# Delta-rule operands on VectorE, bonus products a step later, merged gram masks, and 62 instead of 82 products ahead of the block inverses

## Chip, cores and metric

One Trainium2 chip, one core. The metric is the device time of one execution in microseconds (us). The time before is 968.35 us, the median of 3 runs (964.66 to 969.06).

## What is computed

One layer of a hybrid encoder on 1024 tokens of width 1024, in float32. A normalised input goes through one combined projection (3724 columns), whose pieces feed four branches: A, an mLSTM matrix memory (4 heads of 64); B, causal pooling over trailing windows; C, RWKV-7 time mixing, a delta rule with data-dependent decay; D, forgetting attention. The gated branches are joined by an output projection, and a cross-attention into 256 memory tokens follows. The change touches branch C and, in two small places, branch A:

```python
def step(state, xs):                      # branch C, for every token
    r_t, k_t, v_t, w_t, kk_t, a_t = xs
    sa = jnp.einsum("bhvk,bhk->bhv", state, -kk_t)
    state = state * w_t[:, :, None, :] + sa[..., None] * (kk_t * a_t)[:, :, None, :] \
            + v_t[..., None] * k_t[:, :, None, :]
    return state, jnp.einsum("bhvk,bhk->bhv", state, r_t)
...
bonus = jnp.sum(rh * kh * bonus_u, axis=-1, keepdims=True) * vh
```

## The kernel before

Float32 accuracy comes from three passes: both factors of a product are split into a high and a low part, and a **product** is three matmuls (L137 to L139, hi*hi, lo*hi, hi*lo). A product of the projections has 512 moving columns, or 260 to 264 for the two value projections (`vgemm`).

TensorE's order is the order in which the program is written (`manual_schedule`). The large projections are generators in a list of fillers; `fill(n)` takes n units from the list and puts them at that place in TensorE's stream. A 512-column product counts one unit, a `vgemm` product half a unit. So the small dependent steps of branch C stand in TensorE's queue with fixed numbers of products between them. The other engines' order is set by a scheduler with priorities.

Branch C has these stages, in this order:

- **Preparation** (`cprep`, L512 to L555), one step for each of two halves of the sequence (`hf`) and two pairs of heads (`j`), four steps in all. A step begins on TensorE with the two gate products (tiles `sm`, written by L137 to L139 from `lora` and `sp`); ScalarE takes two tanh (L525, L529); VectorE makes a running sum (L533); ScalarE two exponentials (L535, L537); then the operands are written: `EE` (tiles `t`, `ee`) and `BK` (tile `bk`) by L546 to L549, each on 64 partitions x 512 elements. L546 and L548 run on VectorE, L547 and L549 on GpSimd. L550 makes the input of the bonus on VectorE. After a `yield`, TensorE sums it over channels (L554, the **bonus product**) and VectorE copies the result (L555). The buffers `gc`, `ep`, `ta` and `km` exist once, so a step's first ScalarE operation waits until the step before has read them. The PSUM tiles `sm` have two buffers, used in turn.
- **Gram blocks** (`cgram`, L562): 128 small matmuls (L570) in eight groups; VectorE multiplies each result by a mask (L577, L579) on its way out of PSUM.
- **Inverses** (`cinv`, L588): the masked blocks go to DRAM (`dN`, L585) and come back in another layout (L590); VectorE runs 31 dependent steps (L597, L599) that invert 128 blocks of 32 x 32; the result goes to DRAM (`dTn`, `dTt`, L601, L602) and is read back (L611 to L613) by `tinv`, whose first matmul is L621. Meanwhile TensorE takes `fill(NI)`, `NI = 82`: the projections DQ and DK with the norms of their heads (`rgemm`, L805, L806), and most of the value projection AV.
- **Chain** (`cchain`, L663): 16 dependent steps with up to six units between their parts; what is left of the fillers comes after.

Then the mLSTM: `mpre(i)` (L1024) makes the weights of a block from `e`, loaded from `cd` (L1030), and products L1037; `mlstm(i)` (L1041) has the products L1052 with the state. Both have 64 rows of contraction: the halves of the partitions (`PH[x]`) are two heads.

The transfers in question all stand in SyncE's one queue, in order.

Of the kernel before, what the change touches and what calls it, by code (L numbers as in the profile page):

```python
# [36 lines left out]
def tile_trunk(ctx: ExitStack, tc: tile.TileContext, a, out, dbg=None):  # L37
# [317 lines left out]
    masks = []  # L355
# [157 lines left out]
    def cprep(hf, j):  # L513
        hs, js = slice(hf * 512, (hf + 1) * 512), slice(j * 128, (j + 1) * 128)
        cr, ck = shifted[j], shifted[2 + j]
        if j == 0:
            BON[hf] = cm("bon", [128, 4, 4])
            EG[hf] = cm("eg", [128, 2, 8])
        bk = cm("bk", [128, 8, 2, 64])
        BK[j][hf] = bk  # L520
        ep = c1("ep", [128, 8, 65])
        p = ps("sm", [128, 512])
        mm3(p, lora[0][0:64, js], lora[1][0:64, js], cwa[0][0:64], cwa[1][0:64], True, True)
        gc = c1("gc", [128, 512])
        SC.activation(gc, p, AF.Tanh, bias=col(36 + j), scale=0.5)  # L525
        p = ps("sm", [128, 512])
        mm3(p, lora[0][64:128, js], lora[1][64:128, js], cwa[0][64:128], cwa[1][64:128], True, True)
        ta = c1("ta", [128, 512])
        SC.activation(ta, p, AF.Tanh, bias=col(38 + j), scale=0.5)  # L529
        if hf == 0 and j == 1:  # L530
            csplit(1)
        V.tensor_scalar(gc, gc, 1.0, None, op0=ALU.add)
        V.tensor_tensor_scan(gc, smask.rearrange("p a b -> p (a b)"), gc, 0.0, op0=ALU.mult, op1=ALU.add)  # L533
        G.memset(ep[:, :, 0:1], 1.0)
        SC.activation(ep[:, :, 1:65], v3(gc), AF.Exp, scale=-CDEC)  # L535
        V.tensor_copy(EG[hf][:, j, :], ep[:, :, 64])
        act["cprep"] = SC.activation(gc, gc, AF.Exp, scale=CDEC)  # L537
        kk = KN.pop((hf, j))
        km = c1("km", [128, 512])
        V.tensor_scalar(km, ta, pd[:, 7 + j:8 + j], pd[:, 9 + j:10 + j], op0=ALU.mult, op1=ALU.add)  # L540
        V.tensor_tensor(km, ck[:, hs], km, op=ALU.mult)
        V.scalar_tensor_tensor(ta, ta, 1.0, gc, op0=ALU.add, op1=ALU.mult)
        for x in range(2):
            r = PH[x]
            e = EE[x][hf][r, j]
            V.scalar_tensor_tensor(e[:, :, x, :], v3(kk[r]), -1.0, ep[r, :, 0:64], op0=ALU.mult, op1=ALU.mult)  # L546
            G.tensor_tensor(e[:, :, 1 - x, :], v3(cr[r, hs]), ep[r, :, 1:65], op=ALU.mult)  # L547
            V.scalar_tensor_tensor(bk[r, :, x, :], v3(kk[r]), 0.5, v3(ta[r]), op0=ALU.mult, op1=ALU.mult)  # L548
            G.tensor_tensor(bk[r, :, 1 - x, :], v3(km[r]), v3(gc[r]), op=ALU.mult)  # L549
        V.scalar_tensor_tensor(kk, cr[:, hs], col(44 + j), km, op0=ALU.mult, op1=ALU.mult)  # L550
        yield
        bps = ps("sm", [128, 4, 2])
        for i in range(4):
            T.matmul(bps[:, i, :], kk[:, i * 128:(i + 1) * 128], ones2, start=True, stop=True)  # L554
        V.tensor_copy(BON[hf][:, :, 2 * j:2 * j + 2], bps)  # L555
# [4 lines left out]
    def cgram(hf, n):  # L560
        bq = cc("bq", [128, 8, 2, 128])
        BQ[hf] = bq  # L562
        for cp in range(4):
            pp = [ps(t_, [128, 2, 2, 128]) for t_ in (("cw", "cs") if cp % 2 else ("sm", "sm"))]
            for j in range(2):
                for c2 in range(2):
                    c = cp * 2 + c2
                    for x in range(2):
                        r = PH[x]
                        T.matmul(pp[x][:, j, c2, :], BK[j][hf][r, c].rearrange("p a b -> p (a b)"),  # L570
                                 EE[x][hf][r, j, c].rearrange("p a b -> p (a b)"), start=True, stop=True)
            fill(n)
            for x in range(2):
                r, ro = PH[x], PH[1 - x]
                p = pp[x]
                for j in range(2):
                    V.tensor_tensor(EE[x][hf][ro, j, cp * 2:cp * 2 + 2].rearrange("p c a b -> p c (a b)"), p[ro, j],  # L577
                                    masks[x][ro, None, :].to_broadcast([64, 2, 128]), op=ALU.mult)
                    V.tensor_tensor(bq[r, cp * 2:cp * 2 + 2, j, :], p[r, j],  # L579
                                    masks[x][r, None, :].to_broadcast([64, 2, 128]), op=ALU.mult)  # L580
        for x in range(2):
            for b in range(2):
                q0 = hf * 64 + b * 32 + x * 16
                r0 = x * 64 + b * 32
                SY.dma_start(dN[q0:q0 + 16].rearrange("q s t -> s q t"),  # L585
                             bq[r0:r0 + 32, :, :, r0:r0 + 32].rearrange("p c j t -> p (c j) t"))
# [59 lines left out]
            SC.copy(SV[c - 1][0:64, 1::2, :], p[0:64, :, 64:128])  # L646

    FA, FB, FC = 2, 2, 2
    NI = 82
    BN = {}  # L650

    def cbk(c):
# [128 lines left out]
    def rgemm(c0, b0, r0, gcl=None, lag=None):  # L781
# [32 lines left out]
        def ev(c, p):  # L814
            for hf in range(2):
                u = cur["stg"]("zu", [128, 512])
                us.append(u)
                if hf:
                    V.tensor_scalar(u, p[hf], col(b0 + c), None, op0=ALU.add)  # L819
                else:  # L820
                    SC.activation(u, p[hf], AF.Identity, bias=col(b0 + c))
                if gcl is None:
                    put(2 * c + hf)
            if gcl is not None and c == 0:
                square(0)
# [111 lines left out]
    with tc.manual_schedule(engines={PE}):  # L937
# [11 lines left out]
            csplit(0)  # L949
        fill(5)  # L950
        gs = [cprep(hf, j) for hf in range(2) for j in range(2)]
        for g in gs:
            with tc.issue_after(act["cnorm"].ins):
                next(g)
            if g is gs[-1]:
                act["ln"] = tc.keep_in_program_order(SC.preload_act_table_set("natural_log_exp_and_others"))
            fill(13)
            run(g)
        c1.close()
        fillers += [rgemm(O_DQ, 66, 0, 46, (7, 5, 5, 5)), rgemm(O_DK, 68, 256, 47, (4, 3, 3, 2)), vgemm(O_AV, 264, 0, avd), rgemm(O_AQ, 0, 512)]  # L960
        cc = Pool("cc", {"bq": 2, "n4": 4, "pr": 1, "t11": 1, "sv": 3, "ik": 2, "bn": 2, "w": 1, "uu": 1,
# [63 lines left out]
    def mpre(i):  # L1025
# [5 lines left out]
        V.tensor_tensor(e, e, maskA[:, None, :].to_broadcast([128, 4, 128]), op=ALU.add)  # L1031
        for h in range(4):
            SC.activation(e[:, h, :], e[:, h, :], AF.Exp, bias=gk(0, i, h))
        for x in range(2):
            p = ps("ml", [128, 2, 128])
            for j in range(2):
                T.matmul(p[:, j, :], akT[j][PH[x], ts], aqT[j][PH[x], ts], start=True, stop=True)  # L1037
            V.scalar_tensor_tensor(e[:, x::2, :], p, 0.125, e[:, x::2, :], op0=ALU.mult, op1=ALU.mult)
        return vt, e

    def mlstm(i, vt, e):  # L1041
# [4 lines left out]
        nu = am("nu", [128, 4, 65])  # L1046
        SC.copy(nu, pn)
        if i > 0:
            for x in range(2):
                pi = ps("ml", [128, 2, 65])  # L1050
                for j in range(2):
                    T.matmul(pi[:, j, :], aqT[j][PH[x], ts], Cst[PH[x], j, :], start=True, stop=True)  # L1052
                for j in range(2):
                    h = 2 * j + x
                    V.scalar_tensor_tensor(nu[:, h, :], pi[:, j, :], gk(2, i, h), nu[:, h, :], op0=ALU.mult, op1=ALU.add)
        dn = base("tm", [128, 4])
        SC.activation(dn, nu[:, :, 64], AF.Abs)
        V.tensor_tensor(dn, dn, gk(3, i), op=ALU.max)
# [502 lines left out]
```

## Time and profile before

| what | value |
|---|---|
| median of 3 runs | 968.35 us |
| profiled execution, its own time | 968.87 us |
| its span | 967.0 us |
| mean granted TensorE clock | 0.975 of 2.4 GHz |
| busy, share of the span | PE 94%, PEld 80%, DVE 60%, ACT 43%, POOL 27% |
| chain that ended last | PE 35% of the span, every other engine 2% or less |

The page names PE (TensorE matmuls), PEld (its weight loads), DVE (VectorE), ACT (ScalarE), POOL (GpSimd) and SP (SyncE). A busy matmul's duration overlaps the next one's, so the time that work costs on PE is read from the distance between the starts of rows. A clock of 0.5 means that matmuls ran at 1.2 GHz instead of 2.4. Idle time is given with what ended it.

### The profile page before, as it was taken

How to read it: one execution, taken by the hardware profiler on the slowest of the kernel's cores; microseconds unless marked ns; L12 is line 12 of the kernel's file. 1: busy time of each engine (PE TensorE's matmuls, PEld its weight loads, DVE VectorE, ACT ScalarE, POOL GpSimd, SP SyncE). 2: the span in 40 equal slices, each digit the busy share in tenths (PEclk: the TensorE clock that was granted, in tenths of full speed). 3: DMA queues.
4: the chain of work that ended last, by engine and by line, in shares of the span. 5: the costliest groups of instructions: out<-in, count | busy, mean ns of one | idle time of the engine just before them, and what ended most of it. 6: DMA issues, size and time to landing. Idle time of an engine off the chain costs nothing. (4 is left out here: it accounts for less than half of the span.)

```text
span 967.0 us, 16286 instructions
## 1 busy us (share of the span) xinstructions
PE 911.7 (94%) x6057; PEld 769.8 (80%) x6057; DVE 577.0 (60%) x1290; ACT 419.6 (43%) x974; POOL 264.3 (27%) x270
## 2 busy tenths in 40 slices
PE   6989999797998999999898988999999999999997
PEld 6987887596777887777676766788887888889997
DVE  6873136887698135796378747566666546654226
ACT  6667255231055334654345135445455434443321
POOL 4654223552121224344333452000000000121211
PEclk9999999887999999999999999999999999999999
DMA  7877411102323512332476466634327211125104
GB/s 237 264 229 256 120 46 35 41 12 71 66 85 117 129 29 72 100 104 88 129 155 174 150 213 226 204 102 134 112 77 260 78 33 45 45 93 180 44 2 174
DMA packets 98255, 114.37 MB, mean 118 GB/s; under 512 B 20929, under 2 KB 76801, under 8 KB 98177
## 3 DMA queue, kind: packets, MB, share of 16 engines
q1 hardware_dynamic: 98176, 113.34, 38.3%
q8 instruction: 48, 0.79, 0.4%
q14 instruction: 31, 0.25, 0.1%
HBM read 84.44 MB, written 28.87 MB: 117 GB/s over the span
## 5 line engine op out<-in xcount | busy, mean ns | idle before, releaser
L126 POOL TENSOR_TENSOR wl<-wr,wh 128x512 fp32r<-128x512 f32 (+2 forms) x98 | 140.4, 1435 | 395.4 <-ACT wh L122 380.3
L137 PE MATMUL mm<-h,wh 128*128 128x512 f32 x528 | 221.5, 419 | 3.0 <-DVE zu L754 2.7
L138 PE MATMUL mm<-l,wh 128*128 128x512 f32 x528 | 210.9, 399 | 0.0
L139 PE MATMUL mm<-h,wl 128*128 128x512 f32 x528 | 210.8, 399 | 0.0
L137 PEld LDWEIGHTS mm<-h,wh 128*128 128x128 f32 x528 | 101.0, 191 | 27.7 <-DVE zu L754 3.1
L139 PEld LDWEIGHTS mm<-h,wl 128*128 128x128 f32 x528 | 101.2, 192 | 23.4
L122 ACT CAST wh<-wr 128x512 fp32r<-128x512 f32 (+2 forms) x122 | 74.7, 621 | 100.9 <-PE mm L138 35.4
L138 PEld LDWEIGHTS mm<-l,wh 128*128 128x128 f32 x528 | 101.3, 192 | 17.7 <-issue 0.5
L137 PE MATMUL mm<-wh,act 128*128 128x256 f32 x256 | 71.8, 281 | 0.0
L138 PE MATMUL mm<-wl,act 128*128 128x256 f32 x256 | 71.0, 277 | 0.0
L139 PE MATMUL mm<-wh,act 128*128 128x256 f32 x256 | 70.8, 277 | 0.0
L137 PE MATMUL mm<-h,act 128*128 128x512 f32 x128 | 53.6, 419 | 0.7 <-ACT jk L1305 0.7
L138 PE MATMUL mm<-l,act 128*128 128x512 f32 x128 | 50.4, 394 | 0.0
L139 PE MATMUL mm<-h,act 128*128 128x512 f32 x128 | 50.4, 394 | 0.0
L137 PEld LDWEIGHTS mm<-wh,act 128*128 128x128 f32 x256 | 48.2, 188 | 0.1
L138 PEld LDWEIGHTS mm<-wl,act 128*128 128x128 f32 x256 | 48.1, 188 | 0.0
L139 PEld LDWEIGHTS mm<-wh,act 128*128 128x128 f32 x256 | 48.0, 188 | 0.0
L137 PE MATMUL mm<-wh,h 128*128 128x260 f32 (+1 forms) x128 | 39.4, 308 | 1.5 <-DVE zu L819 1.5
L137 PE MATMUL mm<-mT,wh 128*128 128x256 f32 x128 | 37.5, 293 | 1.4 <-ACT wh L122 1.4
L139 PE MATMUL mm<-mT,wl 128*128 128x256 f32 x128 | 37.1, 290 | 1.6 <-DVE wl L124 1.6
L138 PE MATMUL mm<-wl,h 128*128 128x260 f32 (+1 forms) x128 | 38.3, 299 | 0.0
L139 PE MATMUL mm<-wh,l 128*128 128x260 f32 (+1 forms) x128 | 38.1, 298 | 0.0
(405 smaller groups left out, 2003.5 us busy)
## 6 DMA issues: line engine op xcount, KB each, us to landing
wr<-in_w_in_dram SPq DMA_DIRECT2D x50, 256.0 KB, 2.9
wr<-in_xattn_wkv_dram SPq DMA_DIRECT2D x32, 256.0 KB, 3.8
x<-in_x_dram SPq DMA_DIRECT2D x16, 512.0 KB, 5.0
x<-x1d SPq DMA_DIRECT2D x15, 512.0 KB, 5.6
wr<-in_xattn_wo_dram SPq DMA_DIRECT2D x16, 256.0 KB, 3.1
vwd<-row SPq DMA_DIRECT2D x8, 512.0 KB, 4.0
rT<-zu SPq DMA_DIRECT2D x16, 256.0 KB, 2.3
zT<-zu SPq DMA_DIRECT2D x16, 256.0 KB, 3.2
```

The source lines that it names most:

```text
L122: SC.copy(hi, raw)
L126: G.tensor_tensor(lo, raw, f32(hi), op=ALU.subtract)
L137: T.matmul(o, lh, rh, start=st, stop=False, skip_group_check=skip)
L138: T.matmul(o, lh, rl, start=False, stop=False, skip_group_check=skip)
L139: T.matmul(o, ll, rh, start=False, stop=sp, skip_group_check=skip)
```

## The change

Six edits. (1) The operands of L547 and L549 are made on VectorE. (2) The bonus product of a step is put behind the next step's gate products and 15 units, where it was behind 13 units of its own step; the last one comes after `fill(8)`. (3) The two masks of a gram tile for `j = 0, 1` become one instruction of twice the size. (4) `NI` is 62. (5) The biased evacuation in `rgemm` is on ScalarE for both halves. (6) In `mpre` and `mlstm` both PSUM tiles are taken first, and the matmuls go through `j` outside and `x` inside, so that consecutive ones use different halves of the partitions.

```diff
-            G.tensor_tensor(e[:, :, 1 - x, :], v3(cr[r, hs]), ep[r, :, 1:65], op=ALU.mult)
+            V.tensor_tensor(e[:, :, 1 - x, :], v3(cr[r, hs]), ep[r, :, 1:65], op=ALU.mult)
...
-            G.tensor_tensor(bk[r, :, 1 - x, :], v3(km[r]), v3(gc[r]), op=ALU.mult)
+            V.tensor_tensor(bk[r, :, 1 - x, :], v3(km[r]), v3(gc[r]), op=ALU.mult)
...
-                for j in range(2):
-                    V.tensor_tensor(EE[x][hf][ro, j, cp * 2:cp * 2 + 2].rearrange("p c a b -> p c (a b)"), p[ro, j],
-                                    masks[x][ro, None, :].to_broadcast([64, 2, 128]), op=ALU.mult)
-                    V.tensor_tensor(bq[r, cp * 2:cp * 2 + 2, j, :], p[r, j],
-                                    masks[x][r, None, :].to_broadcast([64, 2, 128]), op=ALU.mult)
+                V.tensor_tensor(bq[r, cp * 2:cp * 2 + 2].rearrange("p c j t -> p j c t"), p[r],
+                                masks[x][r, None, None, :].to_broadcast([64, 2, 2, 128]), op=ALU.mult)
+                V.tensor_tensor(EE[x][hf][ro, :, cp * 2:cp * 2 + 2].rearrange("p j c a b -> p j c (a b)"), p[ro],
+                                masks[x][ro, None, None, :].to_broadcast([64, 2, 2, 128]), op=ALU.mult)
...
-    NI = 82
+    NI = 62
...
-                if hf:
-                    V.tensor_scalar(u, p[hf], col(b0 + c), None, op0=ALU.add)
-                else:
-                    SC.activation(u, p[hf], AF.Identity, bias=col(b0 + c))
+                SC.activation(u, p[hf], AF.Identity, bias=col(b0 + c))
...
-        for g in gs:
+        for n, g in enumerate(gs):
             with tc.issue_after(act["cnorm"].ins):
                 next(g)
...
-            fill(13)
-            run(g)
+            fill(15)
+            if n:
+                run(gs[n - 1])
+        fill(8)
+        run(gs[-1])
...
+        pp = [ps("ml", [128, 2, 128]) for _ in range(2)]
+        for j in range(2):
+            for x in range(2):
+                T.matmul(pp[x][:, j, :], akT[j][PH[x], ts], aqT[j][PH[x], ts], start=True, stop=True)
         for x in range(2):
-            p = ps("ml", [128, 2, 128])
-            for j in range(2):
-                T.matmul(p[:, j, :], akT[j][PH[x], ts], aqT[j][PH[x], ts], start=True, stop=True)
-            V.scalar_tensor_tensor(e[:, x::2, :], p, 0.125, e[:, x::2, :], op0=ALU.mult, op1=ALU.mult)
+            V.scalar_tensor_tensor(e[:, x::2, :], pp[x], 0.125, e[:, x::2, :], op0=ALU.mult, op1=ALU.mult)
```

`mlstm` has the same edit at L1052 (`pi`). The total of products stays the same; they stand elsewhere: ahead of the gram blocks 6 units more (12 products of 260 columns; the fillers run out there, so that the fourth `fill(15)` gives 13 and `fill(8)` nothing), the gram stage has 16 units of 512 columns where it had 6 units of 260 and 10 of 512, between the gram blocks and the inverses 6 products of 512 and 28 of 264 fewer, and in and after the chain 14 units more.

Three places of the instruction streams. VectorE, the operands of the first preparation step (`t` and `bk` are the operands' tiles, `sq` the bonus input, `bon` the copied bonus):

```order
 L546 SCALAR_TENSOR_TENSOR t_1274<-sq_1517,ep_1741 64x8x64
 L542 SCALAR_TENSOR_TENSOR ta_1752<-ta_1752,gc_1746 128x512
+L547 TENSOR_TENSOR t_1274<-rk_1693,ep_1741 64x8x64
+L548 SCALAR_TENSOR_TENSOR bk_1740<-sq_1517,ta_1752 64x8x64
+L549 TENSOR_TENSOR bk_1740<-km_1760,gc_1746 64x8x64
 L546 SCALAR_TENSOR_TENSOR t_1276<-sq_1517,ep_1741 64x8x64
-L548 SCALAR_TENSOR_TENSOR bk_1740<-sq_1517,ta_1752 64x8x64 x2
+L547 TENSOR_TENSOR t_1276<-rk_1693,ep_1741 64x8x64
+L548 SCALAR_TENSOR_TENSOR bk_1740<-sq_1517,ta_1752 64x8x64
+L549 TENSOR_TENSOR bk_1740<-km_1760,gc_1746 64x8x64
 L550 SCALAR_TENSOR_TENSOR sq_1517<-rk_1693,pc,km_1760 128x512
-L555 COPY bon_1738<-sm_1824 128x4x2
```

Four instructions more stand between the gates and the bonus input, and the copy of the bonus has left the step.

The bonus product of the first step, on TensorE before:

```order
L139 MATMUL mm_1705<-h_167,wl_1812 128x512
L554 MATMUL sm_1824<-ones_1288,sq_1517 128x2 x4
L137 MATMUL sm_1832<-sp_1719,lora_1304 128x512
L138 MATMUL sm_1832<-sp_1720,lora_1304 128x512
L139 MATMUL sm_1832<-sp_1719,lora_1305 128x512
```

and now, on TensorE (the gate products that follow are those of the third step) and, second, on VectorE (`sm_1962` is the bonus of the first step, `sq_1558` the bonus input of the second):

```order
L139 MATMUL mm_1925<-wh_1946,l_170 128x260
L554 MATMUL sm_1962<-ones_1288,sq_1517 128x2 x4
L137 MATMUL sm_1972<-sp_1844,lora_1304 128x512
L138 MATMUL sm_1972<-sp_1845,lora_1304 128x512
L139 MATMUL sm_1972<-sp_1844,lora_1305 128x512
L137 MATMUL sm_1978<-sp_1844,lora_1304 128x512
```

```order
L548 SCALAR_TENSOR_TENSOR bk_1830<-sq_1558,ta_1842 64x8x64
L549 TENSOR_TENSOR bk_1830<-km_1854,gc_1836 64x8x64
L550 SCALAR_TENSOR_TENSOR sq_1558<-rk_1699,pc,km_1854 128x512
L555 COPY bon_1738<-sm_1962 128x4x2
L532 TENSOR_SCALAR gc_1976<-gc_1976 128x512
```

The bonus of the first step now stands ahead of the third step's gates, and VectorE copies it only behind the second step's last operand.

SyncE at the gram blocks' way to DRAM and back (`wr` are pieces of weights, `n` the blocks to be inverted), before:

```order
L585 DMA dN<-bq_2238 32x16x32 x4
L115 DMA wr_2799<-in_w_in_dram 128x2x256
L585 DMA dN<-bq_2383 32x16x32 x3
L115 DMA wr_2857<-in_w_in_dram 128x2x256
L585 DMA dN<-bq_2383 32x16x32
L590 DMA n_447_2490<-dN 128x1024
L115 DMA wr_2909<-in_w_in_dram 128x2x264
```

and now:

```order
L584 DMA dN<-bq_2290 32x16x32 x2
L115 DMA wr_2767<-in_w_in_dram 128x2x256
L584 DMA dN<-bq_2290 32x16x32 x2
L584 DMA dN<-bq_2385 32x16x32 x2
L115 DMA wr_2825<-in_w_in_dram 128x2x256
L584 DMA dN<-bq_2385 32x16x32 x2
L115 DMA wr_2877<-in_w_in_dram 128x2x264
L589 DMA n_447_2476<-dN 128x1024
```

The load of the blocks stands behind one piece of weights more than before.


## Rows read from the trace of the kernel before

**Rows 1.** Busy time by stretch: stretch, length, PE, PEld, DVE, ACT, POOL, PEclk, DMA.
```profile
157.00:225.00 68.00, 56.00 (x296) 47.81 (x294) 55.83 (x61) 20.97 (x38) 34.69 (x25) 0.85 0.13 35
253.00:321.00 68.00, 63.99 (x367) 55.65 (x366) 46.50 (x108) 28.74 (x61) 14.38 (x14) 1.00 0.36 102
331.00:454.00 123.00, 121.74 (x1143) 94.71 (x1142) 72.41 (x171) 59.76 (x181) 46.98 (x54) 0.99 0.26 76
470.00:560.00 90.00, 81.69 (x467) 63.65 (x467) 64.77 (x150) 37.91 (x86) 37.27 (x40) 0.96 0.60 156
```

**Rows 2.** Waits of PE, whole span: total us, times, longest.
```profile
PE sm L554 <- DVE sq L550: 11.5, 4, 4.4
...
PE ml L1037 <- DVE e L1038: 3.2, 1, 3.2
PE ml L1052 <- DVE e L1038: 3.0, 4, 1.2
```

**Rows 3.** Timeline of DVE and ACT, preparation: start us, us, engine, line, operation.
```profile
162.47 0.69 DVE L541 TENSOR_TENSOR km<-rk,km 128x512 f32<-128x512 f32 x1
...
164.17 0.68 DVE L546 SCALAR_TENSOR_TENSOR t<-sq,ep 64x512 f32<-64x512 f32 x1
...
168.22 3.35 DVE L548 SCALAR_TENSOR_TENSOR bk<-sq,ta 64x512 f32<-64x512 f32 x2
171.61 1.69 DVE L550 SCALAR_TENSOR_TENSOR sq<-rk,pc,km 128x512 f32<-128x512 f32 x1
...
176.41 0.69 ACT L525 ACTIVATE gc<-sm,pc 128x512 f32<-128x512 f32 x1 [8.97 <-PE sm L139]
...
180.17 1.70 DVE L546 SCALAR_TENSOR_TENSOR t<-sq,ep 64x512 f32<-64x512 f32 x1
```

**Rows 4.** Timeline of POOL, the first preparation step.
```profile
162.74 3.17 POOL L547 TENSOR_TENSOR t<-rk,ep 64x512 f32<-64x512 f32 x2 [7.03 <-ACT ep L535]
...
167.60 3.42 POOL L549 TENSOR_TENSOR bk<-km,gc 64x512 f32<-64x512 f32 x2
```

**Rows 5.** Timeline of PE, the first preparation step.
```profile
160.52 0.39 PE L137 MATMUL mm<-h,wh 128*128 128x512 f32 x1
...
168.19 0.39 PE L137 MATMUL mm<-h,wh 128*128 128x512 f32 x1
...
173.44 1.31 PE L554 MATMUL sm<-ones,sq 128*128 128x2 f32 x8 [4.40 <-DVE sq L550]
```

**Rows 6.** Timeline of DVE and PE: first mask, last gram matmuls, last mask.
```profile
227.33 0.43 DVE L577 TENSOR_TENSOR t<-sm,maskG 64x256 f32<-64x256 f32 x1 [1.08 <-PE sm L570]
...
252.28 0.38 PE L570 MATMUL cs<-ee,bk 64*128 64x128 f32 x2
...
257.54 0.43 DVE L579 TENSOR_TENSOR bq<-cs,maskG 64x256 f32<-64x256 f32 x1
```

**Rows 7.** Timeline of ACT, DVE, SP and PE, from gram blocks to inverses.
```profile
266.02 0.69 ACT L821 ACTIVATE zu<-mm,pc 128x512 f32<-128x512 f32 x1 [1.62 <-PE mm L139]
...
268.60 0.18 DVE L597 TENSOR_TENSOR pr<-n,n 128x31 f32<-128x31 f32 x1
...
302.97 1.03 DVE L600 COPY n<-n 128x1024 f32<-128x1024 f32 x1
...
310.74 0.54 SPq L611 DMA_DIRECT2D t<-dTn  x1
...
321.30 2.11 PE L621 MATMUL sm<-t,bq 32*32 32x32 f32 x64
```

**Rows 8.** DMA issues: form, count, KB each, median us to landing, 255 to 335.
```profile
t<-dTn SPq DMA_DIRECT2D x4, 64.0 KB, 2.6
```

**Rows 9.** Timeline of PE and DVE, the start of the mLSTM.
```profile
463.64 0.72 PE L1037 MATMUL ml<-t,t 64*128 64x128 f32 x8
...
469.35 0.69 DVE L1031 TENSOR_TENSOR e<-e,maskA 128x512 f32<-128x512 f32 x1 [10.50 <-DMA e<-cd]
...
486.64 0.67 PE L1052 MATMUL ml<-Cst,t 64*128 64x65 f32 x8
```

More of the change, by code (lines that the diff above doesn't have):

```diff
@@ L1048, in mlstm @@
         if i > 0:
[L1049 to L1055, printed above, removed]
+            pi = [ps("ml", [128, 2, 65]) for _ in range(2)]
+            for j in range(2):
+                for x in range(2):
+                    T.matmul(pi[x][:, j, :], aqT[j][PH[x], ts], Cst[PH[x], j, :], start=True, stop=True)
+            for h in range(4):
+                V.scalar_tensor_tensor(nu[:, h, :], pi[h % 2][:, h // 2, :], gk(2, i, h), nu[:, h, :], op0=ALU.mult, op1=ALU.add)
         dn = base("tm", [128, 4])
```

## Prediction

> **What bounds the kernel now.** I read the page first: TensorE is busy for 94% of the span and carries the chain that ended last, so time can only come from stretches in which it stands still or runs at the lower clock. The busy time by stretch shows where that is. In the preparation (157 to 225) TensorE is busy for 56.00 of 68 us and its granted clock is 0.85, while VectorE is busy for 55.83 [rows 1]. In the chain it is busy for 121.74 of 123 us, so a product moved there costs its full time [rows 1]. The list of TensorE's waits names the largest: 11.5 us in four waits of the bonus product for its input, L550 [rows 2].
>
> The timeline of VectorE says why L550 is late. The first operand, L546, takes 0.68 us; the same kind of instruction takes 3.35 for two and 1.69 a moment later [rows 3]. At those times GpSimd runs L547 and L549, 3.17 us and 3.42 us for two each [rows 4]. So VectorE loses 1.0 us per instruction while GpSimd works beside it. In the first step that happens to six of its seven operand instructions, from L542 on. The bonus product waits 4.40 us for the result [rows 5].
>
> **The change, part by part.** All of it is set against the profiled execution, 968.87 us, which lies 0.5 above the median. A product of 512 columns costs 0.70: 11 of them lie between the two starts in [rows 5], 7.67 us. One of 260 to 264 columns costs 0.36 by its columns.
>
> *Preparation.* Nine operand instructions of 64 or 128 rows by 512 stand in a step (L542, and two each of L546 to L549). An undisturbed one takes 0.68, the same as a plain product of two tensors on VectorE, 0.69 [rows 3]; consecutive ones overlap a little, so 0.65. Nine take 5.9. From a step's first ScalarE operation to its first operand it is 3.8 (176.41 to 180.17 in [rows 3]). GpSimd keeps the low halves of weights; I count one collision of 1.0 per step, two in the second. Then:
> - step 1: TensorE is the limit. 15 products from 159.8 on, 10.5, and the gates, 1 (six matmuls of 512 columns, two at a time): ScalarE starts step 2 at 171.3 (before: 176.4 [rows 3]).
> - step 2: VectorE is the limit: 3.8 + 5.9, four evacuations of the value tiles at 0.7 as for any 128 x 512, two collisions: 14.7, so 186. TensorE is through its 15 units (11 x 0.70 + 8 x 0.36 = 10.6) and the bonus at 183 and then waits some 3.5 us: the second gate product needs the PSUM buffer of the first step's bonus, and that copy stands behind L550 in VectorE's queue. This wait is new.
> - step 3: TensorE: gates until 187.3, 30 x 0.36 = 10.8, 2 for the lower clock that follows such a wait (a mean of 0.85 over 68 us is 10 us lost for four waits [rows 1, 2]), 0.7 for the bonus: 201.
> - step 4: VectorE: 3.8 + 5.9 + 1.0 + L550 0.7: 212.4. Two bonus products, their copies and the first gram group take 4.3 more by my estimate (the bonus 1.31 in [rows 5] is at the lower clock): the first mask at 216.7 instead of 227.3 [rows 6], 10.6 earlier, with 12 products more behind it.
>
> *Gram blocks.* 64 masks of 0.42 to 0.43 fill VectorE from 227.33 to 257.97 [rows 6]. 256 elements more cost 0.27 (0.69 against 0.42), so 32 masks take 0.69 each, 22.1: the last ends at 238.8, 19.2 earlier. The last gram matmul ends 4.1 ahead of it (four masks and the hand-over), at 234.7; before it was 252.66 [rows 6]: **-17.9**.
>
> *From the last gram matmul to the inverses' first product.* Before 68.6 (252.66 to 321.30 [rows 6, 7]). TensorE now has 50 products of 512, 28 of 264 and eight norms of four matmuls of 256 columns, 0.5 each: 49. The inverses need longer. Before, ScalarE's evacuation came 13.4 and the first of the 31 steps 15.9 after the last gram matmul [rows 6, 7]; now the evacuation comes six products earlier, 4.2, and a second one on ScalarE, 0.7, slips in between: 12.4, and I take 12.6, since the load of the blocks stands behind a piece of weights more. The steps took 34.4 (268.60 to 302.97 [rows 7]), less three evacuations of 0.7 that leave VectorE: 32.3, end at 45. From that end the read that L621 needs was issued 7.8 later [rows 7], and such a read lands in 2.6 [rows 8]. So 45 + 10.4 = 55.3: **-13.3**. TensorE stands for some 6 us in here.
>
> *Moved work.* 28 products of 264 columns come in the chain or after it, where nothing is idle [rows 1]: 28 x 0.36 = **+10.1**.
>
> *Start of the mLSTM.* `e` arrives 10.50 us after VectorE has become idle [rows 9], and TensorE waits 3.2 for it [rows 2]; work behind it at the lower clock costs something more, at most 2 as above. Now 11 units stand behind the chain, 7.7 us, and the load of `e` is ahead of the last evacuations in SyncE's queue: **-4** (0 to -5.2).
>
> *Row halves.* Eight groups of L1037 take 0.72 each and seven of L1052 0.67 [rows 9]. If halves overlap as the gram matmuls do, 2.7 us of TensorE's time go; VectorE is busy for 64.77 of 90 us there and sets part of the pace [rows 1]: **-1** (0 to -2.7). The Trainium skill (TensorEngine Tiling (Array Packing), PSUM Bottleneck) says that tiling speeds up TensorE and not the evacuation of PSUM; by it this term would be nothing and the sum 944. The waits for L1038 [rows 2] lean that way.
>
> The evacuations moved to ScalarE cost nothing beyond the 0.7 named: ScalarE is busy for 28.74 of 68 us there [rows 1].
>
> Sum: -17.9 - 13.3 + 10.1 - 4 - 1 = -26.1, so **943 us**.
>
> **Rivals.**
>
> *The operands' move gives nothing.* If both engines only share one path, VectorE pays for its own product what it paid in waiting: the first mask stays at 227.3, and 10.6 of the gain is lost: 953.5. For it: GpSimd's instructions of 1.6 to 1.7 [rows 4] are themselves stretched. Against it: six blocked instructions cost 6 us a step and four new ones 2.6. The Trainium skill (Perfetto Trace Analysis, Optimizing Scalar/DVE Operations) says that GpSimd and VectorE share an SBUF read port, so that moving operations between those two might not help; that is this rival, and by it the time would be 953.5.
>
> *The inverses take the gain.* With 62 products the reads come no earlier after the gram blocks than before: 310.74 + 2.6 is 60.7 after the last gram matmul [rows 7, 8], 5.4 more than I take, and TensorE, idle for 11, resumes at the lower clock, 2: 950.
>
> *Slower.* The 1.7 us is not GpSimd's doing but that of these operands (64 rows, four of their inputs shared). Then the 36 operand instructions of the four steps cost 1.69 instead of 0.65, 37 us, of which TensorE's work in steps 1 and 3 hides 4: 33 - 26 = 7 slower, 976. It decides from 1.47 us per instruction on. Against it: the first L546 of a step, before GpSimd starts, takes 0.68 [rows 3].
>
> *It does not do what it says*: the order of instructions shows all moves, so only a stage that gives the time back later is left, and the chain has no idle time to absorb it.
>
> **How the numbers follow.** Forecast 0.70, no gain from the move 0.12, the inverses 0.10, slower 0.05, nothing left 0.03. Low end: no collisions and no new wait, 5 less, and both last terms in full, 2.8 less: 935, so 934. High end: the 953.5 with 2 us of an open term: 956. 0.5% (4.8 us) is about what a measurement of this kernel tells from no change. Faster by more than that 0.91, within it 0.04, slower 0.05.
>
> **What would show it.** L546 to L549 at 0.7 us each; the wait for L550 under 2 us, a wait of the third step's gates of 2 to 5 us behind L555; 32 masks of 0.69; the first of the 31 steps some 12.5 us after the last gram matmul; L620 about 31 us earlier than L621 before, and the mLSTM's first product about 21 earlier; no wait of L1036 for `e`. Operands at 1.7 us, or TensorE waiting over 10 us ahead of the inverses, would make it wrong.

## Result and the profile after

The changed kernel takes 954.5 us (median of 4 runs, 949.2 to 958.2) where the kernel before took 966.5 beside it (4 runs): a ratio of 0.9864, 95% interval 0.9832 to 0.9897. Timed again later, beside seven new runs of the kernel before (968.24), it took 951.67: 0.9847 (0.9809 to 0.9885). So it is faster by 12 to 17 us, inside the predicted range, and by about half of the 26 that the sum gave.

The first trace is of an execution of 958.15, the second of the repeat. Both, cut at the same instructions (starts of rows; "gate" is the first L525, "TensorE's end" the end of its last matmul):

| stretch | before | after | repeat | predicted change | measured |
|---|---|---|---|---|---|
| start to gate | 159.6 | 163.0 | 159.2 | 0 | +3.4, -0.4 |
| gate to end of last gram matmul | 93.1 | 79.7 | 79.6 | -17.9 | -13.4, -13.5 |
| to first inverse matmul (L620) | 68.6 | 55.6 | 55.4 | -13.3 | -13.0, -13.2 |
| to first mLSTM matmul L1045 | 154.9 | 165.6 | 166.2 | +6.1 (10.1 - 4) | +10.7, +11.2 |
| to branch D's first transpose (L1246) | 97.4 | 96.8 | 101.7 | -1 | -0.6, +4.3 |
| to last matmul of L1447 | 315.4 | 315.1 | 311.8 | 0 | -0.3, -3.6 |
| to TensorE's end | 71.6 | 74.1 | 74.1 | 0 | +2.5, +2.5 |

Nothing that is changed stands ahead of the gate, so the first row and the differences between the two traces are chance of an execution.

Busy time by stretch, after (columns and stretches as in [rows 1]; a fixed stretch holds somewhat later work now):

```profile
157.00:225.00 68.00, 61.38 (x369) 52.05 (x367) 57.29 (x93) 27.28 (x53) 14.11 (x12) 0.93 0.19 53
253.00:321.00 68.00, 63.83 (x504) 56.70 (x504) 42.45 (x98) 34.04 (x80) 11.92 (x13) 0.95 0.36 105
331.00:454.00 123.00, 119.12 (x998) 93.01 (x997) 67.56 (x157) 56.63 (x162) 49.03 (x58) 0.97 0.27 83
```

In the preparation TensorE is busy for 5.4 us more (369 matmuls instead of 296) and its clock is 0.93 instead of 0.85; GpSimd is down from 34.7 to 14.1. But the clock fell in the two later stretches, from 1.00 to 0.95 and from 0.99 to 0.97.

TensorE's waits, after, whole span (us, times, longest; answers to [rows 2]):

```profile
PE sm L554 <- DVE sq L550: 3.8, 1, 3.8
PE sm L805 <- DVE ysb L161: 3.5, 3, 2.5
PE cs L683 <- DVE w L671: 3.3, 1, 3.3
...
PE ml L1052 <- DVE e L1038: 2.6, 4, 1.1
```

The wait for L550 is one instead of four, 3.8 us instead of 11.5. The wait of L683 in the chain is new. That of the mLSTM's product for `e` (3.2) is gone.

Timeline, after: an undisturbed operand, the fourth step, masks and the last gram matmul (start us, us, engine, line; answers to [rows 3 to 6]):

```profile
179.41 0.68 DVE L546 SCALAR_TENSOR_TENSOR t<-sq,ep 64x512 f32<-64x512 f32 x1
...
209.06 1.77 POOL L126 TENSOR_TENSOR wl<-wr,wh 128x512 fp32r<-128x512 f32 x1 [2.30 <-ACT wh L122]
...
209.57 1.80 DVE L548 SCALAR_TENSOR_TENSOR bk<-sq,ta 64x512 f32<-64x512 f32 x1
...
211.16 1.37 POOL L126 TENSOR_TENSOR wl<-wr,wh 128x512 fp32r<-128x512 f32 x1 [0.34 <-ACT wh L122]
...
211.29 1.78 DVE L549 TENSOR_TENSOR bk<-km,gc 64x512 f32<-64x512 f32 x1
...
214.44 1.68 POOL L126 TENSOR_TENSOR wl<-wr,wh 128x512 fp32r<-128x512 f32 x1 [1.91 <-ACT gates L740]
214.90 1.76 DVE L549 TENSOR_TENSOR bk<-km,gc 64x512 f32<-64x512 f32 x1
...
217.59 1.84 PE L554 MATMUL sm<-ones,sq 128*128 128x2 f32 x8 [3.82 <-DVE sq L550]
...
220.31 2.08 PE L570 MATMUL sm<-t,bk 64*128 64x128 f32 x16 [0.35 <-ACT sv L643]
...
222.42 0.68 DVE L576 TENSOR_TENSOR bq<-sm,maskG 64x512 f32<-64x512 f32 x1 [1.49 <-PE sm L570]
...
228.13 1.16 PE L570 MATMUL sm<-t,bk 64*128 64x128 f32 x16
...
242.41 0.27 PE L570 MATMUL cs<-ee,bk 64*128 64x128 f32 x1
...
244.76 0.68 DVE L578 TENSOR_TENSOR ee<-cs,maskG 64x512 f32<-64x512 f32 x1
```

The operand takes 0.68, and 1.8 in each place where GpSimd makes the low half of a piece of weights beside it. The list of fillers is empty there, so TensorE stands 3.82 us, and the bonus and the first gram group then run at 1.2 GHz: a group of 16 matmuls takes 2.08, and 1.16 once the clock is back.

Timeline, after, from the inverses into the chain and the mLSTM (answers to [rows 7, 9]):

```profile
255.99 1.26 DVE L596 TENSOR_TENSOR pr<-n,n 128x31 f32<-128x31 f32 x1 [1.14 <-DMA n<-dN]
...
288.67 1.03 DVE L599 COPY n<-n 128x1024 f32<-128x1024 f32 x1
...
290.09 0.39 PE L805 MATMUL sm<-ysb,onesr 128*128 128x256 f32 x1 [2.49 <-DVE ysb L161]
...
298.10 0.28 PE L139 MATMUL mm<-wh,l 128*128 128x264 f32 x1
298.31 1.19 PE L620 MATMUL sm<-t,bq 32*32 32x32 f32 x32
299.69 1.19 PE L620 MATMUL sm<-t,bq 32*32 32x32 f32 x32 [0.19 <-DMA t<-dTn]
...
301.20 0.42 PE L138 MATMUL mm<-wl,h 128*128 128x264 f32 x1
...
416.19 1.33 ACT L921 ACTIVATE t<-n,pc 128x512 f32<-128x512 f32 x2 [5.26 <-DMA n<-rT]
416.95 0.75 DVE L924 SCALAR_TENSOR_TENSOR t<-n,pc,t 128x511 f32<-128x511 f32 x1 [6.07 <-ACT t L921]
...
417.73 0.42 DVE L671 COPY w<-cw 128x256 f32<-128x256 f32 x1
...
418.21 0.69 PE L683 MATMUL cs<-w,n 64*64 64x64 f32 x8 [3.26 <-DVE w L671]
...
456.11 0.72 PE L1036 MATMUL ml<-t,t 64*128 64x128 f32 x8
```

TensorE works up to L620 and waits only 0.19 us there for the second read of the inverses; its longest wait on this way is 2.49 us, for a norm (L805). Behind L620 a matmul of 264 columns takes 0.42, and 0.28 at 2.4 GHz. The chain's copy L671 stands in VectorE's queue behind a multiply-add of the mLSTM's convolution (`aconv`), which waits for a load.

### The profile page after: what moved, and what is told of

It is laid out like the page before. It is cut to its first block, busy times and chain, and to the rows that moved or that the text cites. A ratio compares the mean times of both kernels' runs of the same rounds, so it can differ in the third digit from the quotient of the medians.

```text
span 956.3 us, 16250 instructions
## 1 busy us (share of the span) xinstructions
PE 907.8 (95%) x6057; PEld 766.3 (80%) x6057; DVE 559.7 (59%) x1266; ACT 424.9 (44%) x982; POOL 236.5 (25%) x254
## 5 line engine op out<-in xcount | busy, mean ns | idle before, releaser
L126 POOL TENSOR_TENSOR wl<-wr,wh 128x512 fp32r<-128x512 f32 (+2 forms) x98 | 137.8, 1407 | 430.6 <-ACT wh L122 389.6
L137 PE MATMUL mm<-h,wh 128*128 128x512 f32 x528 | 220.6, 418 | 3.0 <-DVE zu L753 2.7
L137 PEld LDWEIGHTS mm<-h,wh 128*128 128x128 f32 x528 | 100.8, 191 | 27.5 <-DVE zu L753 3.2
L137 PE MATMUL mm<-wh,act 128*128 128x256 f32 x256 | 72.8, 284 | 0.0
L137 PE MATMUL mm<-h,act 128*128 128x512 f32 x128 | 53.6, 419 | 0.3 <-ACT jk L1304 0.3
L137 PEld LDWEIGHTS mm<-wh,act 128*128 128x128 f32 x256 | 48.3, 189 | 0.1
L137 PE MATMUL mm<-wh,h 128*128 128x260 f32 (+1 forms) x128 | 38.9, 304 | 0.9 <-DVE v L480 0.8
L137 PE MATMUL mm<-mT,wh 128*128 128x256 f32 x128 | 37.7, 295 | 1.4 <-ACT wh L122 1.4
L1493 DVE TENSOR_TENSOR o<-mm,gb 128x256 f32<-128x256 f32 x32 | 13.6, 425 | 43.4 <-ACT junk L1492 43.1
```

The costliest lines, as they stand in the source:

```text
L126: G.tensor_tensor(lo, raw, f32(hi), op=ALU.subtract)
L137: T.matmul(o, lh, rh, start=st, stop=False, skip_group_check=skip)
L1493: V.tensor_tensor(o3[i][:, gs], p, xog[:, gs], op=ALU.mult)
```

## Experiments

Theory A: GpSimd's instructions stretch VectorE's, and each edit ahead of the inverses gives its part. Theories B and C, formed after the result, say where the missing half went: into new waits with the lower clock behind them (B), and into the wait for the inverses, whose end hangs on VectorE and DRAM (C). Ratios are to the kernel before, timed on the same chip; the changed kernel has 0.9864 and 0.9847. The fifth edit was not undone in any run.

**One edit undone, four kernels.**

```diff
 u1_operands
-            V.tensor_tensor(e[:, :, 1 - x, :], ...)
+            G.tensor_tensor(e[:, :, 1 - x, :], ...)
-            V.tensor_tensor(bk[r, :, 1 - x, :], ...)
+            G.tensor_tensor(bk[r, :, 1 - x, :], ...)
 u2_bonus
-            fill(15)
-            if n:
-                run(gs[n - 1])
-        fill(8)
-        run(gs[-1])
+            fill(13)
+            run(g)
 u3_masks
-                V.tensor_tensor(bq[r, cp * 2:cp * 2 + 2]..., p[r], ...)
+                for j in range(2):
+                    V.tensor_tensor(bq[r, cp * 2:cp * 2 + 2, j, :], p[r, j], ...)
...
 u4_ni82
-    NI = 62
+    NI = 82
```

> The changed kernel with the first edit undone: the operands of L547 and L549 back on GpSimd, all else as changed. Theory A (GpSimd's instructions stretch VectorE's): VectorE's operands take up to 1.7 us again, the way from the first gate operation to the first mask, 59.4 us in the changed kernel, grows by 5 to 9 us, TensorE waits for the bonus input again, and the time is 5 to 10 us above the changed kernel's 954.5. Rival (the move gives nothing, VectorE pays for its own products what it paid in waiting): that way stays within 2 us of 59.4, and the time within 2 us of 954.5.

957.1 us, 0.9878 (0.9847 to 0.9908). Gate to first mask is 67.1 us, 7.7 more: theory A's size. The wait has another name, for the evacuation of the value tiles (TensorE's waits of u1, one line):

```profile
PE mm L137 <- DVE v L480: 7.9, 1, 7.9
```

Gate to TensorE's end is 793.7 against 786.9 and 788.8, so 5 to 7 of the 7.7 arrive there by the trace. By the ratios it is 1 to 3 us, and their intervals overlap.

> The changed kernel with the second edit undone: each bonus product in its own step behind 13 units. Theory A (TensorE's wait for the bonus input is what the later place removes): TensorE waits for L550 in every step again, 8 to 11 us in all, the way from the first gate operation to the first mask is 64 to 68 instead of 59.4, and the time is 4 to 8 us above 954.5. Rival (with the operands fast, VectorE sets the pace of the steps, and the place of the bonus product does not matter): the way is 58 to 61, the time within 2 us of 954.5.

956.3 us, 0.9860 (0.9837 to 0.9883): no difference. The way is 64.5 and the waits for L550 7.5 us, nearly theory A's sizes, but the time did not rise. Six units fewer now stand ahead of L620 in all. The way from the last gram matmul to it is 51.2 instead of 55.6, with 2.0 us of idle time instead of 3.8 and a clock of 1.00 instead of 0.97, and the units come back ahead of the mLSTM (30.5 instead of 25.5).

> The changed kernel with the third edit undone: 64 masks of 256 elements a row instead of 32 of 512. Theory A (VectorE sets the pace of the gram blocks when the masks are single): 64 masks of 0.42 to 0.43 fill 27.4 us, the last mask ends 27 to 29 us after the first one starts (23.0 in the changed kernel), and the time is 4 to 6 us above 954.5. Rival (TensorE's eight groups with their 16 products, 21.4 us, and not the masks, set the pace): under 25 us and less than 2 us more time.

955.2 us, 0.9843 (0.9816 to 0.9869): no difference. The masks fill 27.6 us, as theory A has it. The last gram matmul comes only 2.0 later after the first one, since TensorE's own groups take 22.4 here; the trace has 791.3 from gate to end, 2.5 to 4.4 more.

> The changed kernel with the fourth edit undone: 82 units ahead of the inverses instead of 62, so that 40 products of 264 columns leave the chain and what is behind it. Theory of the prediction (28 fewer products give 13.3 ahead of the inverses and 4 at the start of the mLSTM, and cost 10.1 in the chain): 5 to 8 us above 954.5. Rival B (moved products give and cost the same, and the 62 brought two new stalls: the lower clock behind the wait of L805, 2 us, and the wait of L683 in the chain with the lower clock behind it, 6 us, against 5 us at the start of the mLSTM): no wait of L683, and the time is 0 to 5 us below 954.5.

952.0 us, 0.9812 (0.9781 to 0.9843), not slower than the changed kernel; gate to end 786.9, the same. So the 5 to 8 us that were expected by the prediction fall. From the last gram matmul to L620 it is 70.2 instead of 55.6, and the way from there to the mLSTM is 149.3 instead of 165.6: what the 20 units cost in one place they give in the other. The wait for `e` at the mLSTM's start is 0.5 here too, so its going was not the work of this edit alone.

**Repeat and row halves.** c_after is the changed kernel. u6_rows has the two PSUM tiles and their matmuls one after the other, at L1036 and at L1052:

```diff
-        pp = [ps("ml", [128, 2, 128]) for _ in range(2)]
-        for j in range(2):
-            for x in range(2):
-                T.matmul(pp[x][:, j, :], ...)
+        for x in range(2):
+            p = ps("ml", [128, 2, 128])
+            for j in range(2):
+                T.matmul(p[:, j, :], ...)
```

> The changed kernel itself, as the mark for the runs beside it: 954 to 958 us. The way from the first gate operation to the end of the last matmul, 786.9 us in its first trace, repeats within 1 us, with 3.4 of L683's wait in the chain, 3.8 of the wait for L550 and 74.1 from the last matmul of L1447 to the end, if these belong to the kernel; if they were chance of one execution, they differ.

951.67 us, 0.9847. The waits for L550 (3.7) and L683 (3.2) and the 74.1 repeat; gate to end is 788.8, 1.8 more, with 5 us more in the mLSTM (its waits of L1052 for `e` are 5.0 instead of 2.6) and 3.3 less behind it.

> The changed kernel with the sixth edit undone: the mLSTM takes its two PSUM tiles one after the other, and the matmuls of a half stand together. Theory A (alternating halves do not overlap, since a group of eight still takes 0.71 to 0.72 us in the changed kernel; the edit is worth nothing): within 2 us of the changed kernel. Prediction on record (the edit gives 1, at most 2.7): 1 to 2.7 slower. Side question: the way from the last matmul of L1447 to the end is 74.1 us in the changed kernel and in the four with one edit undone, and 71.6 in the kernel before. If the sixth edit sets it, it is 71.6 here.

951.07 us, 0.9832 (0.9802 to 0.9863): no difference, the edit is worth nothing. A group of L1036 takes 0.72 in either form. The last stretch is 74.1, so this edit does not set it.

Theory A has the worth right and the reason wrong: the halves do overlap, and they did in the order before. There one group had to take its halves one after the other, and the four rows of a half alone took 0.71 us (kernel before):

```profile
469.32 0.71 PE L1037 MATMUL ml<-t,t 64*128 64x128 f32 x4
```

Eight rows of both halves take no longer, 0.72 in the kernel before [rows 9] and in u6, where the matmuls of a half stand together:

```profile
451.45 0.72 PE L1036 MATMUL ml<-t,t 64*128 64x128 f32 x8
```

The gram matmuls show how: those of two halves start 0.01 us apart, and the next pair 0.11 later (changed kernel):

```profile
231.01 0.27 PE L570 MATMUL cw<-t,bk 64*128 64x128 f32 x1
231.02 0.27 PE L570 MATMUL cs<-t,bk 64*128 64x128 f32 x1
231.12 0.27 PE L570 MATMUL cw<-t,bk 64*128 64x128 f32 x1
231.13 0.27 PE L570 MATMUL cs<-t,bk 64*128 64x128 f32 x1
```

**The wait in the chain.** f1_aconv keeps the convolution's multiply-adds of its last two tiles behind the chain's copy L671, f4_behind692 behind the chain's last operation of a step, L692:

```diff
-        V.tensor_copy(w, wy)
+        act["w"] = V.tensor_copy(w, wy)
...
+                with tc.issue_after(act["w" if jt > 1 else "cnorm"].ins):
                 for d in range(1, 4):
```

> The changed kernel with one order more: for the last two of the four tiles of the convolution, VectorE's multiply-adds L924 stand behind the chain's copy L671, not ahead of it. Theory B (with 62 units the projection AK ends later, its load comes late, and the copy L671, for which TensorE waits 3.3 us, stands in VectorE's queue behind a multiply-add that waits for that load): the wait of L683 goes, with the lower clock behind it, the chain is 4 to 6 us shorter than 128.2, and the time 4 to 6 us less. Rival (TensorE's waits in the chain are filled by the units that follow anyway, or the multiply-adds are then late for the mLSTM): the chain is shorter but the way from its end to the mLSTM longer, less than 2 us gained.

951.97 us, 0.9844 (0.9805 to 0.9883): nothing. The wait is not gone but moved to the next copy (TensorE's waits of f1):

```profile
PE cs L689 <- DVE uu L685: 3.8, 2, 2.9
```

> The changed kernel with VectorE's multiply-adds L924 of the last two tiles of the convolution behind the chain's last operation of the step, L692, where f1 had them behind its first, L671, and L685 then waited in the same way (3.8 us at L689). Theory B (a chain's copy stands in VectorE's queue behind a multiply-add whose load comes late; behind L692 the load has landed before the next copy is due): waits of TensorE for L671 and L685 under 1.5 us in all, the chain 122 to 125 instead of 128.2 to 128.9, the time 3 to 6 us less than the changed kernel's. Rival (the late load still blocks the next copy, or the convolution then ends late and the mLSTM waits for it): the same waits at another place, less than 2 us gained.

953.12 us, 0.9836 (0.9808 to 0.9865): nothing. The waits for L671 and L685 are 1.9 in all, but the chain takes 127.8. Its trace has stretches at 1.2 GHz in the chain that no wait explains; the rows are in the last section. So theory B's 4 to 6 us for this wait fall: its 3.3 us are there, but removing it gave no time that can be measured.

**The wait ahead of the inverses.** f2_fill and g1_fill_ni76 (which has both parts of the diff):

```diff
+            if g is gs[-1]:
+                fillers.append(rgemm(O_DQ, 66, 0, 46, (7, 5, 5, 5)))
             fill(15)
...
-        fill(8)
+        fill(4)
...
-        fillers += [rgemm(O_DQ, 66, 0, 46, (7, 5, 5, 5)), rgemm(O_DK, ...
+        fillers += [rgemm(O_DK, ...
 g1 alone
-    NI = 62
+    NI = 76
```

> The changed kernel with the projection DQ put into the list ahead of the fourth preparation step, so that the fourth run of 15 units is full and 4 units stand ahead of the last bonus product (6 products of 512 columns, 4.2 us, that the changed kernel has between the gram blocks and the inverses; 12 products of 264 columns take their place there). Theory B (TensorE stands for 3.8 us at the last bonus product because the list runs out, and the gram blocks then begin at the lower clock, 2.5 us): no wait of more than 1 us for L550, the first gram matmul no more than 1.5 later, the gram blocks 2 us shorter, and 4 to 7 us less time. Rival (VectorE, not TensorE, sets the gram blocks' and the inverses' end, so what is done earlier only lengthens a later wait): less than 2 us gained.

951.9 us, 0.9841 (0.9810 to 0.9872): nothing gained. All that was said of the gram blocks is there: no wait for L550, clock 1.00, and gate to last gram matmul 76.7 instead of 79.6. But VectorE's 31 steps then end 127.5 after the gate, and 126.4 in the repeat of the changed kernel: they begin later after the gram blocks (15.0 instead of 13.1) and take 2.1 longer. TensorE waits 5.0 us at L620. The rival holds. Windows of f2: last gram matmul to the steps' end, to L620, to the chain's first matmul, the chain:

```profile
236.02:286.81 50.79, 47.40 (x244) 40.22 (x245) 37.62 (x93) 28.30 (x58) 10.48 (x10) 0.97 0.29 87
286.81:291.75 4.94, 4.94 (x42) 4.81 (x40) 2.09 (x4) 1.31 (x5) 0.00 (x0) 1.00 0.88 306
291.75:309.71 17.96, 12.94 (x175) 12.58 (x175) 1.37 (x2) 2.40 (x5) 3.59 (x4) 0.71 0.36 78
309.71:434.79 125.08, 124.59 (x1163) 98.17 (x1161) 70.10 (x169) 61.15 (x189) 48.74 (x55) 0.97 0.23 73
```

> As f2 (DQ ahead of the fourth preparation step), with 76 instead of 62 units ahead of the inverses. Theory C (TensorE's time saved ahead of the inverses came back as a wait, since the inverses' end hangs on VectorE's 31 steps and the way through DRAM; f2 waited 5.0 us for the read t<-dTn and ran at the lower clock for some 8 us behind it; 14 units, 28 products of 264 columns or 10 us, fill that wait): no wait of L620, from the end of the gram blocks to the chain's first matmul 74 to 77 us with 28 products more in it than f2's 73.7, the chain and what follows 9 to 10 shorter, the time 5 to 9 us less than f2's. Rival (moved products give and cost the same, as between 82 and 62 units): within 2 us of f2's.

943.57 us (942.95 to 945.25), 0.9741 (0.9710 to 0.9772): the fastest kernel of the study, 8.3 us less than f2 and 25 less than the kernel before. The same four windows of g1:

```profile
237.73:287.93 50.20, 46.09 (x246) 38.85 (x246) 37.49 (x93) 28.12 (x58) 10.48 (x10) 1.00 0.29 88
287.93:303.03 15.10, 15.10 (x121) 14.56 (x119) 3.69 (x9) 5.20 (x17) 4.22 (x4) 1.00 0.60 169
303.03:312.69 9.66, 9.66 (x154) 8.35 (x154) 2.35 (x3) 1.79 (x4) 2.34 (x4) 1.00 0.54 140
312.69:431.31 118.62, 115.16 (x1121) 90.22 (x1119) 69.72 (x168) 62.18 (x183) 48.86 (x54) 1.00 0.26 81
```

From the last gram matmul to the chain it is 75.0 with 28 products more, and 73.7 in f2: 10 us of work in 1.3. There is no wait at L620, and the clock is 1.00 throughout. This part of theory C holds. From the chain's first matmul to L1045 it is 140.3 instead of f2's 146.9, 6.5 less where 9 to 10 were expected: the chain is shorter by about the work that has left it, but what stands behind it is not (21.7 and 21.8 us, with 5 products fewer). From there to L1246 g1's trace is 6.4 shorter, though both kernels do the same work there. So the 8.3 us are clear of noise, but how they divide over the stages is not shown.

> As g1, with the order of f4 on VectorE, the sixth edit undone, and the second projection's norms put off to 5 and 7 units behind their squares instead of 4 and 3 (TensorE waited 3.5 us for them, L805). Theory C and B together: none of the waits of L554, L620, L683 and L805 over 1 us, and the way from the first gate operation to the end of the last matmul 772 to 778 us, where the changed kernel has 787 to 789; the time 940 to 946. Rival (each wait that goes comes back at the next place that hangs on VectorE or on a load): 780 to 785, the time 948 to 952.

953.32 us (945.66 to 956.78), 0.9827 (0.9775 to 0.9879): the improvements do not add, and the rival holds. The waits of L554 and L620 are gone, but that of L683 is back with 3.8 us, the chain takes 125.4 instead of g1's 118.6 at a clock of 0.94, and L804 waits 1.9 for its split, which now comes later. One of its four executions took 945.66. The chain also has two stretches of 3.4 us at 1.2 GHz (from 330.8 and from 341.0) with no wait ahead of them. g2 has three changes more than g1, and which of them brought the wait back no run shows.

**The first edit alone.** The kernel before with L547 and L549 on VectorE, and nothing else.

```diff
-            G.tensor_tensor(e[:, :, 1 - x, :], ...)
+            V.tensor_tensor(e[:, :, 1 - x, :], ...)
-            G.tensor_tensor(bk[r, :, 1 - x, :], ...)
+            V.tensor_tensor(bk[r, :, 1 - x, :], ...)
```

> The kernel before with the first edit alone: the operands of L547 and L549 on VectorE, the rest as before. Theory A (GpSimd's instructions stretch VectorE's; the operands come sooner, but each bonus product still stands behind 13 units of its own step): TensorE's waits for L550 fall from 11.5 to 6 to 8 us, the way from the first gate operation to the first mask from 67.7 to 64 to 65, and the time by 3 to 5 us, if nothing later takes it. Rival (the move gives nothing): waits of 10 to 13, 67 to 69, no difference. Side question: from the last matmul of L1448 to the end the kernel before took 71.6 in its one trace, and the eight kernels with the change or most of it 73.9 to 74.1. If the change costs that 2.4, it is 71.6 here; if it is a matter of the chip, 74.

961.81 us, 0.9922 (0.9894 to 0.9951): 6.7 us faster. The waits for L550 are 8.0 in three, gate to first mask 64.7. The rival that the move gives nothing falls. The time gains more than the 3 to 5 us that theory A gave. The trace is 7.5 shorter from the gate to the end: 4.4 of this at the last gram matmul, 1.4 of which are lost again up to L620 and 1.4 won up to L1045, and 3.3 behind L1246, where this edit changes nothing and the two traces of the changed kernel differ as much. So the share of the operands is 3 to 4.4 us by the trace. The last stretch is 71.6.

## Why the prediction was right in direction and its sum too large

- **Operands on VectorE: right.** L546 and L547 take 0.68 undisturbed, as put, and the edit alone gives 6.7 us (a ratio of 0.9894 to 0.9951), of which the traces place 3 to 4.4 where the operands stand. One reading was off: of the first step's six operand instructions five are stretched, not six of seven; in the second step it is all six. The rival "the operands' move gives nothing" (0.12) is out, and so is "slower" (0.05), which needed 1.47 us each. The Trainium skill (Perfetto Trace Analysis, Optimizing Scalar/DVE Operations) says that such a move might not help, as the two engines share a read port; that they disturb each other the rows show, but here the disturbed engine was the one waited for, and the move did help.
- **Preparation and gram blocks: -17.9 put, -13.4 measured.** Taken from the gate, steps 2, 3 and 4 began within 2 us of the times given. The failed step is the fourth: "3.8 + 5.9 + 1.0 + L550 0.7". The 1.0 was one collision with GpSimd; there were four (L540, L548, L549, L549), and L550 ended 1.6 later than put, after allowing for the late start of this run. TensorE waited 3.8 where "under 2" was said, and began the gram blocks at 1.2 GHz. And the gram blocks were taken as VectorE's, the last matmul 4.1 ahead of the last mask: TensorE's eight groups set the pace, and it was 2.8 ahead. The masks themselves took the 0.69 put. The new wait of the third step's gates, put at 3.5 us behind L555, is 1.0 and stands behind ScalarE's L525, which waits for L549 to be through with `gc`.
- **Last gram matmul to L620: -13.3 put, -13.0 measured, in part by luck.** The first of the 31 steps comes after 13.3 (12.6 put), the copy that ends them begins after 46.0 (45), L620 after 55.6 (55.3). But "TensorE stands for some 6 us in here" failed: it is idle for 3.8, 3.5 of it for the norms (L805), runs at 1.2 GHz for 3.4 us behind the last of these, and comes to L620 by its own work, where the second read keeps it for 0.2. The rival "the inverses take the gain" is out with it: L620 did not come after 60.7, nor was TensorE idle for 11, though its 950 lies near the measured time.
- **Moved work and start of the mLSTM: +10.1 - 4 put, +10.7 to 11.2 measured.** The start of the mLSTM did come 4.6 sooner than its work: it takes 25.5 instead of 22.8 with 10 or 11 products of 512 columns, 7.3 us, more in it. What failed is that nothing was put for a lower clock behind L620 and for a new wait in the chain. The way from L620 to the chain takes 11.9 at a clock of 0.86, and 10.5 in the two kernels that ran the same products at 1.00 (u1, f1); the chain has 4.1 us of idle time instead of 1.3, and a clock of 0.97 instead of 0.99. With 82 units the time is the same (u4), so the terms that go with the fourth edit, -13.3 + 10.1 - 4 = -7.2, are worth nothing here: TensorE did not stand at L620, so a product taken out of that way only costs its time later.
- **Row halves: -1 put, 0 measured** (u6). The halves do overlap as the gram matmuls do; what failed is that "2.7 us of TensorE's time go", since they overlapped in the kernel before too (0.72 for both halves, 0.71 for one alone). The Trainium skill (TensorEngine Tiling (Array Packing), PSUM Bottleneck) says that tiling speeds up TensorE and not the evacuation of PSUM, and by that rule the term was nothing; but TensorE was not sped up, so no run here shows whether PSUM would have held the gain back.
- **The sum.** From the gate on, -26.1 was put and -14.1 measured in the first trace. Of the 12 missing, 4.5 lie in the preparation and the gram blocks, 4.6 between L620 and the mLSTM, 2.5 in the last stretch, whose cause is open, and the rest in small terms. Undoing any one of the five edits tried costs at most some 3 us by the ratios, and none of this is clear of noise, though the trace shows the first three edits' own sizes (7.7, 5.1 and 4.6 us at the masks). For the operands these us do reach L620: it comes 142.3 after the gate in u1's trace and 135.3 and 135.0 in the changed kernel's. Of the masks' 4.6 us about 1 does. In the changed kernel TensorE waits 0.2 us at L620, so theory C does not say where its missing half went. It says why a further gain ahead of the inverses gave nothing in f2: the steps end 50.8 us after the last gram matmul there, and the read that TensorE waits for lands some 11 us later. g1 puts work into that way and takes 943.6 us. That this is the 943 that the prediction gave to the change itself is chance, since it takes two edits more.

Still open: which part of the loss in the chain is the wait of L683 and which the clock. f1 and f4 changed the wait and gained nothing, and g1 has neither the wait of L683 nor a clock below 1.00 in the chain, but its chain also has fewer products in it.

## What to carry to other kernels

When a dependent path through another engine and DRAM (here the inverses) sets when TensorE can go on, earlier arrival is worth nothing until independent products are moved into that path; size them by the wait that the trace then shows, no sooner. Expect a wait for an input to cost its length and often a lower clock behind it (the 3.8 us at L550 did, the 2.7 us of L137 at 555.3 us in the same trace did not), and look for an empty list of fillers at the end of a stage. On VectorE's queue an instruction that waits for a load holds up every copy behind it, and moving it behind one copy can move the wait to the next (f1).

## What was not expected

- **The clock falls without a wait.** In f4 no row of this piece of the chain has idle time before it, yet behind 64 matmuls of 32 x 32 (L620) and the chain's eight of 64 columns the matmuls of 512 columns take 0.63 instead of 0.39: they run at 1.2 GHz (timeline of f4, TensorE):

```profile
321.91 2.11 PE L620 MATMUL sm<-t,bq 32*32 32x32 f32 x64
323.95 1.10 PE L669 MATMUL cw<-sv,t 128*128 128x64 f32 x8
324.86 0.47 PE L137 MATMUL mm<-h,wh 128*128 128x512 f32 x1
325.18 0.46 PE L138 MATMUL mm<-l,wh 128*128 128x512 f32 x1
325.43 0.63 PE L139 MATMUL mm<-h,wl 128*128 128x512 f32 x1
```

  The changed kernel itself has both. In its first trace, and then in the repeat, the third of these matmuls:

```profile
328.98 0.40 PE L139 MATMUL mm<-h,wl 128*128 128x512 f32 x1
```

```profile
325.10 0.63 PE L139 MATMUL mm<-h,wl 128*128 128x512 f32 x1
```

  So the same kernel loses this or not from one execution to the next.
- **The last stretch takes 71.6 or 73.9 to 74.1 us.** It has the same 628 matmuls at the same clock of 1.00 in every trace, 113 or 118 ns apart. Kernel before, b1 and f4 have the short form, all others the long one, the changed kernel in both its traces. b1, f4 and g1 were timed on one chip, and f4 has the change, so it is neither the change nor the chip; the cause is open, and it is worth 2.5 us. Windows of the changed kernel, and then of f4:

```profile
875.83:949.91 74.08, 74.08 (x628) 73.77 (x626) 25.39 (x70) 19.77 (x71) 14.17 (x15) 1.00 0.18 61
```

```profile
871.73:943.33 71.60, 71.59 (x628) 71.28 (x626) 25.28 (x70) 19.78 (x71) 14.20 (x15) 1.00 0.18 64
```

- **Executions of one kernel differ in the mLSTM.** From L1045 to its last group the mLSTM takes 74.5 us in one trace of the changed kernel and 79.8 in the other, 73.0 to 81.2 over all kernels. Its mean clock there is 0.98 and 0.94, and TensorE's waits of L1052 for `e` are 2.6 and 5.0; what sets this off is open.
